# A two-layer encoder trunk on one core: x loaded first, modulation blocks pair by pair, norms summed on all partitions by TensorE, modulation sums held behind the norms

## The chip, the core and the metric

The kernel runs on one core of one Trainium2 chip. The metric is the device time of one execution in microseconds (us), from runs on the chip; smaller is better. The engines are named as the profile names them: PE is TensorE's matrix product and PEld its weight load, DVE is VectorE, ACT is ScalarE, POOL is GpSimd, SP is SyncE, which here only issues DMAs, in order.

## The reference

A sequence of 256 tokens of width 2048 (float32) goes through two layers, and then through a last norm with a gain. In each layer every sub-layer is modulated by six vectors that come from one conditioning vector `c`:

```python
cond = silu(c)
mod = cond @ w_ada[l] + b_ada[l]            # 2048 x 12288: six vectors of 2048
sh_a, sc_a, g_a, sh_m, sc_m, g_m = split(mod, 6)

h = rmsnorm(x) * (1 + sc_a) + sh_a
proj = h @ w_in[l]                          # queries, keys, values, latents
...                                         # 4 differential heads, 8 latent heads
x = x + g_a * (concat(out_a, out_b) @ w_o[l])

h = rmsnorm(x) * (1 + sc_m) + sh_m
x = x + g_m * (square(relu(h @ w_mlp_in[l])) @ w_mlp_out[l])     # 2048 -> 8192 -> 2048
```

`rmsnorm(x)` is `x * rsqrt(mean(x*x) + 1e-6)` over the 2048 features of a token. The two latent vectors of the attention (512 and 256 wide) have a norm with a gain as well.

## The kernel before

**Layout.** `x` stays in on-chip memory for the whole kernel as 16 tiles of 128 features by 256 tokens (features on partitions). Two neighbouring tiles make a *pair*; loops over features run over 8 pairs. A weight matrix comes in blocks of 128 partitions by 2048 columns (1 MiB), or in smaller ones.

**Precision by two parts.** A float32 number is written as hi + lo, both in a format that TensorE takes at its full rate. `weights` (L131) loads a raw block, ACT writes hi (L140), DVE writes lo = raw - hi (L141); the products are hi by hi, hi by lo and lo by hi (`mac`, L173). Raw blocks take turns in 5 buffers, hi and lo in 4 each. In layer 0's first product, six of the eight pairs (`WHOLE`) skip the split and use a float32 product (L233), of which the trace records two per tile; their weights load straight into hi and lo buffers (L222).

**The modulation.** `w_ada` is 192 blocks of 1 MiB. Each is multiplied by `cond` and summed along its columns by one DVE operation (L291), whose result is 128 entries of one of the six vectors; a small operation adds the bias (L305, L307). A block uses one of the 5 raw buffers. `ada` (L310) loads and sums at the place where it stands. Elsewhere a block is loaded now and then: each call of `weights` adds `rate` to a credit, loads a block for each whole credit, and queues the sums of the blocks loaded earlier behind its own last subtraction, by a dependency that only orders instructions (`after`, L294).

**The start.** `setup` (L323) loads `c` and small tables, issues four modulation blocks, `x` in four DMAs, sums up the squares of `x` (ACT squares, DVE adds them up, L470 and L471), and then issues ten more blocks (`LEAD`). The vectors sh_a and sc_a take 32 blocks, four for each pair. In `norm_then_by_k` (L528) the loop over the pairs asks for the blocks that its pair needs and that are not there yet (`ada_need`), modulates the pair, and multiplies it with its rows of `w_a` for all 12 column tiles, which accumulate in 6 PSUM banks. Between the pairs of layer 0 stand pieces of set-up work (`fills`: the relative bias and the rotary tables).

**The norm.** `rstd` (L474) turns sums of squares into 1/rms. The squares, tokens on columns, are the stationary operand and a single column of ones is multiplied with them (L482): the result has tokens on partitions, 128 x 1 for each half. ACT takes the root (L486), DVE the reciprocal of 2 columns (L487) and the product with the identity (L491), and TensorE multiplies this diagonal by ones (L492), which puts the 256 values on all partitions, in PSUM. The norms read it there, the first of the kernel reads a copy in on-chip memory (L534). It is called nine times: for four norms over `x` inside the layers, four latent norms and the last one.

**The modulated pair.** `modulated` (L495): DVE forms x times sc times 1/rms (L502), ACT adds sh and rounds to hi (L503), DVE adds sh and subtracts hi (L504). For a whole pair ACT writes the sum in float32 as well (L508).

**The order** of instructions on each engine is set when the program is built, by a planner that goes by the order of the program and its own estimate of when inputs and buffers are ready. Every engine then works through its own list in order.

Of the kernel before, what the change touches and what calls it, by code (L numbers as in the profile page):

```python
# [92 lines left out]
LEAD = 10  # L93
# [7 lines left out]
class Trunk:  # L101
    def __init__(self, ctx, tc, io):
        self.nc, self.tc, self.io = tc.nc, tc, io
        pool = lambda name, bufs, **k: ctx.enter_context(tc.tile_pool(name=name, bufs=bufs, **k))
        self.cp = pool("cp", 1)
        self.wp = pool("wp", 4)
        self.up = pool("up", 40)
        self.tp = pool("tp", 6)
        self.sp = pool("sp", 8)
        self.pp = pool("pp", 8, space=bass.MemoryType.PSUM)  # L110
        self.ada_todo, self.ada_here, self.rate, self.credit = [], [], 0.0, 0.0
        self.n = 0
# [18 lines left out]
    def weights(self, src, width=2048):  # L131
# [11 lines left out]
        self.ada_sums(ins)  # L143
# [179 lines left out]
    def setup(self):  # L323
# [132 lines left out]
    def sumsq(self, acc, val, alone=False):  # L456
# [8 lines left out]
        if acc is None:  # L465
            t = self.u("acc")
            nc.scalar.activation(t, val, AF.Square)
            return [t[:, 0], t[:, 1], t]
        t = self.t("sqx")
        nc.scalar.activation(t, val, AF.Square)  # L470
        nc.vector.tensor_tensor(acc[2], acc[2], t, ALU.add)  # L471
        return acc

    def rstd(self, acc, n):  # L474

        nc = self.nc
        ps = [self.bank("pn") for _ in range(2)]
        r = self.s("rms")
        acc = acc[:2] + acc[3:]
        for i, a in enumerate(acc):  # L480
            for t in range(2):
                nc.tensor.matmul(  # L482
                    ps[t][:, 0, :1], a[:, t * P : (t + 1) * P], self.ones[:, :1], start=i == 0, stop=i == len(acc) - 1
                )
        for t in range(2):
            nc.scalar.activation(r[:, t : t + 1], ps[t][:, 0, :1], AF.Sqrt, bias=self.eps, scale=1.0 / n)  # L486
        nc.vector.reciprocal(r, r)  # L487
        d = self.tp.tile([P, T], F32, tag="t", name=self.name("diag"))
        for t in range(2):
            c = slice(t * P, (t + 1) * P)  # L490
            nc.vector.tensor_scalar(d[:, c], self.ident, r[:, t : t + 1], None, ALU.mult)  # L491
        nc.tensor.matmul(ps[0][:, 1], self.ones, d, start=True, stop=True)  # L492
        return ps[0][:, 1]

    def modulated(self, r, k, sh, sc, whole):  # L495

        nc = self.nc
        t = self.t("ht")
        out = [self.parts("h") for _ in range(2)]
        for i, (hi, lo, _) in enumerate(out):  # L500
            c = slice(k + i, k + i + 1)
            nc.vector.scalar_tensor_tensor(t[:, i], self.x[:, k + i], sc[:, c], r, ALU.mult, ALU.mult)  # L502
            nc.scalar.activation(hi, t[:, i], AF.Identity, bias=sh[:, c])  # L503
            nc.vector.scalar_tensor_tensor(lo, t[:, i], sh[:, c], hi.bitcast(F32), ALU.add, ALU.subtract)  # L504
        if whole is not None:
            f = self.u("hf")
            for i in range(2):
                nc.scalar.activation(f[:, i], t[:, i], AF.Identity, bias=sh[:, k + i : k + i + 1])  # L508
                whole.append(f[:, i])
        return out  # L510
# [17 lines left out]
    def norm_then_by_k(self, l, acc, sh, sc, src, n, nwhole, fill=(), early=()):  # L528
# [445 lines left out]
```

## Time and profile before

| what | value |
|---|---|
| median of three runs | 2258.67 us (2252.15 to 2260.86) |
| the profiled execution | 2257.36 us |
| its span, first to last instruction | 2255.5 us |
| PE busy | 2191.2 us, 97% |
| DVE busy | 1668.4 us, 74% |
| ACT busy | 1124.8 us, 50% |
| moved by DMA | 585.57 MB, 260 GB/s on average |

The median is over unprofiled runs; the span and everything below it come from the one profiled execution. A busy time is a sum over the whole span, in which stages with different limits lie side by side. Rows of groups read: line, engine, operation, out<-in with the shapes, count | busy us, mean ns of one | idle time of the engine just before them, with what ended it. Rows of the timeline read: start, length, engine, line, operation, and in brackets the idle time before it and what ended it.

### The profile page before, as it was taken

To read this page: it belongs to the slowest core of one execution; us is meant where nothing else is said; L and a number is where in the kernel's file an instruction comes from. 1 tells how busy PE (TensorE), PEld (TensorE's weight loads), DVE (VectorE), ACT (ScalarE), POOL (GpSimd) and SP (SyncE) were. 2 spreads that over 40 slices of the span, in tenths; PEclk is the share of its full clock that TensorE was granted. 3 is DMA by queue.
4 is the path that set the end of the run, shared out by engine and by line. 5 is a ranking of instruction groups with operands and counts; after the bars stand their busy time and mean duration, and the time that the engine had idled before them with its cause. 6 is when DMAs were issued, how large, how long until landed. Compare 5 with 4: busy or idle time off the path is not lost.

```text
span 2255.5 us, 33717 instructions
## 1 busy us (share of the span) xinstructions
PE 2191.2 (97%) x13644; PEld 1967.6 (87%) x13644; DVE 1668.4 (74%) x2275; ACT 1124.8 (50%) x1660; POOL 1.9 (0%) x10
## 2 busy tenths in 40 slices
PE   3999999999999999999999999999999999999998
PEld 1899889998888888888889998999888888888887
DVE  7889878888888878878888786675655565565565
ACT  2655664455455355345445465544635534544553
POOL 0000000000000000000000000000000000000000
PEclk9999999999999999999999999999999999999999
DMA  9988678898888887888869766665555555555552
GB/s 365 357 314 319 257 278 313 309 340 326 300 317 311 302 316 288 332 315 315 301 249 345 265 231 225 237 227 183 203 186 186 177 201 187 187 187 187 187 187 75
DMA packets 85262, 585.57 MB, mean 260 GB/s; under 512 B 9457, under 2 KB 9841, under 8 KB 20593
## 3 DMA queue, kind: packets, MB, share of 16 engines
q1 hardware_dynamic: 85106, 583.42, 70.2%
q8 instruction: 107, 1.75, 0.3%
q14 instruction: 49, 0.40, 0.0%
HBM read 581.28 MB, written 2.10 MB: 259 GB/s over the span
## 4 chain that ended last, share of the span: by engine, by line
PE 94%; DVE 3%; DMA 1%; ACT 1%; issue 0%; SPq 0%; DVEq 0%; ACTq 0%
PE ps L196 38%; PE ps L197 20%; PE pk L176 5%; PE pk L177 5%; PE pk L178 5%; PE pk L233 3%; PE ps L177 3%; PE ps L176 3%; PE ps L178 3%; PE pv L249 1%; PE pv L247 1%; PE pv L248 1%; DVE ada L291 1%; PE po L828 1%; PE psm L863 1%; PE pom L880 1%
## 5 line engine op out<-in xcount | busy, mean ns | idle before, releaser
L141 DVE TENSOR_TENSOR lo<-raw,hi 128x1024 fp32r<-128x1024 f32 (+1 forms) x728 | 861.4, 1185 | 452.7 <-ACT hi L140 450.4
L140 ACT ACTIVATE hi<-raw 128x1024 fp32r<-128x1024 f32 (+1 forms) x728 | 746.9, 1028 | 855.8 <-PE ps L196 563.4
L196 PE MATMUL ps<-hid,hi 128*128 128x512 f32 x2048 | 721.2, 397 | 0.0
L196 PE MATMUL ps<-h,hi 128*128 128x512 f32 x1664 | 584.9, 396 | 0.0
L197 PE MATMUL ps<-hid,lo 128*128 128x256 f32 x2048 | 574.6, 281 | 0.0
L197 PE MATMUL ps<-h,lo 128*128 128x256 f32 x1664 | 466.9, 281 | 0.0
L196 PEld LDWEIGHTS ps<-hid,hi 128*128 128x128 f32 x2048 | 384.4, 188 | 93.7 <-DVE hid L170 0.5
L291 DVE SCALAR_TENSOR_TENSOR ada<-ada,cond 128x2048 f32<-128x2048 f32 x192 | 437.9, 2283 | 6.9 <-ACT cond L335 6.9
L197 PEld LDWEIGHTS ps<-hid,lo 128*128 128x128 f32 x2048 | 386.9, 189 | 0.0
L196 PEld LDWEIGHTS ps<-h,hi 128*128 128x128 f32 x1664 | 312.2, 188 | 74.9
L197 PEld LDWEIGHTS ps<-h,lo 128*128 128x128 f32 x1664 | 314.4, 189 | 0.0
L176 PE MATMUL pk<-h,hi 128*128 128x256 f32 x752 | 213.4, 288 | 3.5 <-ACT h L503 3.5
L177 PE MATMUL pk<-h,hi 128*128 128x256 f32 x752 | 214.3, 286 | 0.2 <-DVE h L504 0.2
L178 PE MATMUL pk<-h,lo 128*128 128x256 f32 x752 | 214.1, 285 | 0.0
L734 DVE SCALAR_TENSOR_TENSOR x<-ps,mod,x 128x256 f32<-128x256 f32 x224 | 108.2, 483 | 61.1 <-PE ps L197 56.9
L176 PEld LDWEIGHTS pk<-h,hi 128*128 128x128 f32 x752 | 146.0, 197 | 5.1 <-ACT h L503 5.1
L177 PEld LDWEIGHTS pk<-h,hi 128*128 128x128 f32 x752 | 146.5, 195 | 0.4 <-DVE h L504 0.4
L178 PEld LDWEIGHTS pk<-h,lo 128*128 128x128 f32 x752 | 146.4, 195 | 0.0
L233 PE MATMUL pk<-hf,w 128*128 128x256 f32 x288 | 65.9, 390 | 18.2 <-DMA w<-in_w_a 18.2
L233 PEld LDWEIGHTS pk<-hf,w 128*128 128x128 f32 x288 | 56.4, 197 | 27.1 <-ACT h L503 18.9
L746 ACT ACTIVATE relu<-sum 128x512 f32<-128x512 f32 x52 | 32.9, 632 | 69.9 <-DVE sum L741 69.9
L176 PE MATMUL ps<-h,hi 128*128 128x256 f32 x192 | 55.6, 289 | 0.0
(207 smaller groups left out, 2474.2 us busy)
## 6 DMA issues: line engine op xcount, KB each, us to landing
raw<-in_w_m SPq DMA_DIRECT2D x232, 1024.0 KB, 4.9
ada<-in_w_ada SPq DMA_DIRECT2D x192, 1024.0 KB, 5.0
raw<-in_w_ob SPq DMA_DIRECT2D x24, 1024.0 KB, 5.7
raw<-in_w_m SPq DMA_DIRECT2D x32, 768.0 KB, 4.6
raw<-in_w_dv SPq DMA_DIRECT2D x16, 1024.0 KB, 5.1
raw<-in_w_a SPq DMA_DIRECT2D x20, 768.0 KB, 6.3
raw<-in_w_t SPq DMA_DIRECT2D x12, 1024.0 KB, 5.1
w<-in_w_a SPq DMA_DIRECT2D x24, 384.0 KB, 5.8
```

Source lines behind the costliest of these rows:

```text
L140: nc.scalar.activation(hi, v, AF.Copy)
L141: ins = nc.vector.tensor_tensor(lo, v, hi.bitcast(F32), ALU.subtract)
L176: mm(ps, hi, x[0], start=first, stop=False, skip_group_check=shared)
L177: mm(ps, hi, x[1], start=False, stop=False, skip_group_check=shared)
L178: mm(ps, lo, x[0], start=False, stop=last, skip_group_check=shared)
L196: mm(ps.rearrange("p a b -> p (a b)"), hi, both, start=k == 0, stop=False)
L197: mm(ps[:, 0], lo, x, start=False, stop=k == nk - 1)
L233: self.nc.tensor.matmul(ps, w[i][:, j * P : j * P + P], whole[i], start=first, stop=last, skip_group_check=True)
L247: mm(ps, xh, hi, start=first and k == 0, stop=False)
L291: ins = nc.vector.scalar_tensor_tensor(w, w, 1.0, self.cond, ALU.mult, ALU.mult, accum_out=acc[:, i : i + 1])
L734: self.nc.vector.scalar_tensor_tensor(x, ps[i][:, j], g[:, m + i : m + i + 1], x, ALU.mult, ALU.add)
L746: self.nc.scalar.activation(r, ps, AF.Relu)
```

## The change

1. `setup` issues the four DMAs of `x` first and then four modulation blocks. The ten blocks of `LEAD` are not loaded there any more; each pair's blocks come when the loop over the pairs reaches it.
2. The squares of `x` in `setup` are kept as 16 tiles and not added up on DVE.
3. `rstd` makes all 128 columns of ones the stationary operand and multiplies the squares with it, 256 columns at a time: the sum lands on all partitions at once. The root and the reciprocal work on 128 x 256, and the result stays in on-chip memory, in one of the six buffers named "t". The diagonal and its product are gone, and so is the copy for the first norm.
4. `modulated`: DVE multiplies x by 1/rms only, ACT applies scale and shift together, once rounded to hi and once in float32 (for every pair now), and DVE subtracts the two.
5. In the first pair after a norm, the modulation sums that `weights` queues are ordered behind the last subtraction of that pair's modulation, and no longer behind the subtraction of the weights (`hold`).

```diff
-LEAD = 10
...
+        self.hold = None
...
-        self.ada_sums(ins)
+        self.ada_sums(self.hold or ins)
...
-        self.ada(4)
         for q in range(4):
             nc.sync.dma_start(self.x[:, 4 * q : 4 * q + 4], io["xT"][:, 4 * q : 4 * q + 4])
-        acc = None
+        self.ada(4)
+        acc = []
         for k in range(0, NK, 2):
-            acc = self.sumsq(acc, self.x[:, k : k + 2])
-        self.ada(LEAD)
+            t = self.u("sq")
+            nc.scalar.activation(t, self.x[:, k : k + 2], AF.Square)
+            acc += [t[:, 0], t[:, 1]]
         return acc
...
     def rstd(self, acc, n):
         nc = self.nc
-        ps = [self.bank("pn") for _ in range(2)]
-        r = self.s("rms")
-        acc = acc[:2] + acc[3:]
+        ps = self.bank("pn")[:, 0]
         for i, a in enumerate(acc):
-            for t in range(2):
-                nc.tensor.matmul(
-                    ps[t][:, 0, :1], a[:, t * P : (t + 1) * P], self.ones[:, :1], start=i == 0, stop=i == len(acc) - 1
-                )
-        for t in range(2):
-            nc.scalar.activation(r[:, t : t + 1], ps[t][:, 0, :1], AF.Sqrt, bias=self.eps, scale=1.0 / n)
+            nc.tensor.matmul(ps, self.ones, a, start=i == 0, stop=i == len(acc) - 1)
+        r = self.tp.tile([P, T], F32, tag="t", name=self.name("rstd"))
+        nc.scalar.activation(r, ps, AF.Sqrt, bias=self.eps, scale=1.0 / n)
         nc.vector.reciprocal(r, r)
-        d = self.tp.tile([P, T], F32, tag="t", name=self.name("diag"))
-        for t in range(2):
-            c = slice(t * P, (t + 1) * P)
-            nc.vector.tensor_scalar(d[:, c], self.ident, r[:, t : t + 1], None, ALU.mult)
-        nc.tensor.matmul(ps[0][:, 1], self.ones, d, start=True, stop=True)
-        return ps[0][:, 1]
+        return r

     def modulated(self, r, k, sh, sc, whole):
         nc = self.nc
         t = self.t("ht")
+        f = self.u("hf") if whole is not None else self.t("hf")
         out = [self.parts("h") for _ in range(2)]
         for i, (hi, lo, _) in enumerate(out):
             c = slice(k + i, k + i + 1)
-            nc.vector.scalar_tensor_tensor(t[:, i], self.x[:, k + i], sc[:, c], r, ALU.mult, ALU.mult)
-            nc.scalar.activation(hi, t[:, i], AF.Identity, bias=sh[:, c])
-            nc.vector.scalar_tensor_tensor(lo, t[:, i], sh[:, c], hi.bitcast(F32), ALU.add, ALU.subtract)
+            nc.vector.tensor_tensor(t[:, i], self.x[:, k + i], r, ALU.mult)
+            for z in (hi, f[:, i]) if whole is None else (f[:, i], hi):
+                nc.scalar.activation(z, t[:, i], AF.Identity, bias=sh[:, c], scale=sc[:, c])
+            ins = nc.vector.tensor_tensor(lo, f[:, i], hi.bitcast(F32), ALU.subtract)
...
-        return out
+        return out, ins
...
     def norm_then_by_k(self, l, acc, sh, sc, src, n, nwhole, fill=(), early=()):
         r = self.rstd(acc, D)
-        if early:
-            ps, r = r, self.tp.tile([P, T], F32, tag="t", name=self.name("rstd"))
-            self.nc.scalar.activation(r, ps, AF.Copy)
...
-            h += self.modulated(r, k, self.mod[l, sh], self.mod[l, sc], whole)
+            new, ins = self.modulated(r, k, self.mod[l, sh], self.mod[l, sc], whole)
+            h += new
+            self.hold = None if p else ins
             self.by_k(banks, [src[l, p, b] for b in range(2)], h, k, NK, 2 * n, whole)
+            self.hold = None
```

More of the change, by code (lines that the diff above doesn't have):

```diff
@@ L467, in sumsq @@
             nc.scalar.activation(t, val, AF.Square)
-            return [t[:, 0], t[:, 1], t]
+            self.acc2 = t
+            return [t[:, 0], t[:, 1]]
         t = self.t("sqx")
         nc.scalar.activation(t, val, AF.Square)
-        nc.vector.tensor_tensor(acc[2], acc[2], t, ALU.add)
+        nc.vector.tensor_tensor(self.acc2, self.acc2, t, ALU.add)
         return acc
@@ L501, in modulated @@
             c = slice(k + i, k + i + 1)
[L502 to L504 removed]
+            nc.vector.tensor_tensor(t[:, i], self.x[:, k + i], r, ALU.mult)
+            for z in (hi, f[:, i]) if whole is None else (f[:, i], hi):
+                nc.scalar.activation(z, t[:, i], AF.Identity, bias=sh[:, c], scale=sc[:, c])
+            ins = nc.vector.tensor_tensor(lo, f[:, i], hi.bitcast(F32), ALU.subtract)
         if whole is not None:
[L506 to L509, printed above, removed]
[L510 removed]
+            whole += [f[:, 0], f[:, 1]]
+        return out, ins
     def latent(self, vals, g):
```

## The prediction, made before the run

> **What bounds the kernel now.** I read the profile page first, then what TensorE waits for, then busy time by stretch, and last the timelines of the first 120 us and of the norms. The page: TensorE is busy for 2191.2 of 2255.5 us, so only 64 us of idle time can be won, beside the time it runs at a lower clock.
>
> ```profile
> span 2255.5 us, 33717 instructions
> PE 2191.2 (97%) x13644; PEld 1967.6 (87%) x13644; DVE 1668.4 (74%) x2275; ACT 1124.8 (50%) x1660; POOL 1.9 (0%) x10
> ```
>
> The list of TensorE's waits names the places (total us, times, longest):
>
> ```profile
> PE pk L233 <- DMA w<-in_w_a: 18.2, 1, 18.2
> PE pn L482 <- DVE acc L471: 15.3, 1, 15.3
> PE pn L492 <- DVE diag L491: 7.3, 4, 2.7
> ```
>
> The first two lie in the first 49 us; the third is the chain of the four big norms. By stretch (length, then busy us of PE, PEld, DVE, ACT, POOL, then granted clock, DMA share, GB/s):
>
> ```profile
> 10.50:28.00 17.50, 1.87 (x8) 1.78 (x8) 16.13 (x19) 5.89 (x10) 0.00 (x0) 1.00 1.01 423
> 28.00:48.00 20.00, 1.19 (x2) 0.50 (x2) 19.46 (x32) 3.90 (x10) 0.00 (x0) 1.00 0.98 394
> 28.00:62.00 34.00, 14.48 (x53) 11.82 (x53) 32.07 (x54) 9.94 (x21) 0.00 (x0) 1.00 0.90 350
> 62.00:118.00 56.00, 56.00 (x257) 48.49 (x257) 50.20 (x96) 33.32 (x58) 0.53 (x1) 1.00 0.94 361
> 118.00:168.00 50.00, 49.84 (x376) 48.36 (x376) 42.74 (x52) 25.46 (x35) 0.00 (x0) 1.00 0.83 317
> 168.00:250.00 82.00, 78.26 (x582) 73.88 (x582) 76.54 (x143) 45.48 (x83) 0.00 (x0) 1.00 0.78 295
> 428.00:441.00 13.00, 9.02 (x51) 8.25 (x50) 11.03 (x20) 5.31 (x11) 0.00 (x0) 0.74 0.86 302
> ```
>
> Until 48 us TensorE has nothing to do; from 62 us it is full. But VectorE is 90% busy from 28 to 62 us and 93% from 168 to 250 us, and DMA tops out near 423 GB/s. The start can be shortened only as far as these two allow. The last row is a norm: TensorE idle for 4 of 13 us, at a mean clock of 0.74.
>
> **The start, step by step.** These rows of the timeline (start, length) set it:
>
> ```profile
> 9.90 31.64 SPq L283 DMA_DIRECT2D ada<-in_w_ada  x10
> 41.59 15.53 SPq L222 DMA_DIRECT2D w<-in_w_a  x10
> ...
> 16.73 0.63 ACT L467 ACTIVATE acc<-x 128x512 f32<-128x512 f32 x1 [6.23 <-DMA x<-in_xT]
> ...
> 48.72 13.23 PE L233 MATMUL pk<-hf,w 128*128 128x256 f32 x48 [18.19 <-DMA w<-in_w_a]
> ...
> 61.92 10.61 PE L233 MATMUL pk<-hf,w 128*128 128x256 f32 x48
> ...
> 118.05 10.52 PE L233 MATMUL pk<-hf,w 128*128 128x256 f32 x48
> ```
>
> Before, the ten LEAD blocks sit in SP's in-order queue ahead of the first weights of w_a, which are issued at 41.59. Removing LEAD lets SP issue x (4 DMAs), 4 blocks, 4 weight tiles, then each pair's 4 blocks and 4 tiles. Nothing on POOL's queue moves. x used to land behind four 1 MiB blocks, with its first quarter used at 16.73; without that 4.2 MB at 423 GB/s (9.9 us) it is there at about 7. The four blocks land when the old x did: 16.7 us plus the other three quarters, 1.6 MB at 423 GB/s, 20.4 us. The last of them needs one sum (2.28 us), a small add and ACT's pass (0.50): the first product can start at about 25, say 26 to be safe with the norm's own steps between the sums. Its four weight tiles (1.6 MB, 3.7 us) start to land just behind the blocks. So TensorE could start 48.7 - 26 = 22.7 us earlier.
>
> How much is kept? From 61.92 to 118.05 TensorE needs 14.0 us per pair, bias work included. Per pair, DMA must now bring four blocks and 1.57 MB, 5.77 MB, 13.6 us at 423 GB/s: just enough. VectorE is tighter. It worked 16.13 + 32.07 + 50.20 + 42.74 + 76.54 = 217.7 us from 10.5 to 250. The durations for what changes (busy, mean ns):
>
> ```profile
> L291 DVE SCALAR_TENSOR_TENSOR ada<-ada,cond 128x2048 f32<-128x2048 f32 x192 | 437.9, 2283 | 6.9 <-ACT cond L335 6.9
> ...
> L471 DVE TENSOR_TENSOR acc<-acc,sqx 128x512 f32<-128x512 f32 x7 | 4.8, 691 | 0.6
> ...
> L502 DVE SCALAR_TENSOR_TENSOR ht<-x,mod,pn 128x256 f32<-128x256 f32 x48 | 21.1, 475 | 2.4 <-PE pn L492 2.2
> ...
> L449 DVE TENSOR_TENSOR cc<-cc,rr 128x256 f32<-128x256 f32 x1 | 0.4, 426 | 0.0
> L448 DVE TENSOR_SCALAR cc<-rr 128x256 f32<-128x256 f32 x1 | 0.3, 293 | 0.0
> ...
> L307 DVE TENSOR_TENSOR mod<-macc,vec 128x2 f32<-128x2 f32 x64 | 9.8, 154 | 0.2
> ...
> L740 ACT ACTIVATE sum<-ps 128x256 f32<-128x256 f32 x104 | 38.1, 367 | 0.0
> L503 ACT ACTIVATE h<-ht,mod 128x256 fp32r<-128x256 f32 x64 | 29.4, 500 | 37.7 <-DVE ht L502 37.5
> ```
>
> The seven adds of squares go (-4.8; TensorE does them in 16 products of two records each, 2 x 10.52 / 48 = 0.44 us, while it has nothing else). Each of the 16 modulated tiles of this stage trades two operations of 0.48 for two of 0.43 (-1.7). In three norms (the first and two latents) the 2-column reciprocal and the diagonal (0.16 + 0.48) give way to one reciprocal of 128x256.
>
> **The reciprocal** of 256 columns is in no row; the nine of 2 columns are (least, median, largest ns):
>
> ```profile
> L487 DVE RECIPROCAL rms<-rms x9: 158/159/167, 28.4 to 2244.8; 128x2 f32<-128x2 f32 x9
> ```
>
> From below it costs what the cheapest 256-column operation does, 0.29 us. From above: the slowest one against the 154 ns of a 2-column add is 6.5 ns for a column, 256 x 6.5 + 160 = 1.8 us. By the median it is 2.5 ns a column, 0.8 us. The rows are coarse (5 ns decide), so I take the middle of the last two, 1.3, and keep 0.29 and 1.8.
>
> So VectorE's work until 250 us becomes 217.7 - 4.8 - 1.7 - 1.9 + 3.9 = 213.2 us, and it can begin only when the first block lands, at 12.9 (20.4 less three blocks of 2.5). If it keeps the density of 168 to 250, 76.54/82 = 0.933, it needs 228.5 us and ends at 241.4: the stage gains 8.6 us. With the density of 28 to 48 (0.973) the gain is 18; with the mean of 28 to 250 (201.6/222 = 0.908) it is 2.3. I take 8.6, because the long dense stretch is the nearest thing to what comes.
>
> **The norms.** One of them, last square to first product:
>
> ```profile
> 1159.96 0.42 ACT L462 ACTIVATE sqa<-x 128x256 f32<-128x256 f32 x1 [0.26 <-DVE x L734]
> ...
> 1160.71 2.28 DVE L291 SCALAR_TENSOR_TENSOR ada<-ada,cond 128x2048 f32<-128x2048 f32 x1
> ...
> 1162.92 0.16 DVE L487 RECIPROCAL rms<-rms 128x2 f32<-128x2 f32 x1
> ...
> 1163.74 1.19 PE L492 MATMUL pn<-diag,ones 128*128 128x256 f32 x2 [2.71 <-DVE diag L491]
> ...
> 1166.05 1.65 PE L176 MATMUL pk<-h,hi 128*128 128x256 f32 x6 [1.11 <-ACT h L503]
> ```
>
> A modulation sum runs on VectorE just when the reciprocal is due; the hold puts it behind the first pair's last subtraction. The new chain from the end of the last square: product with ones 0.71 (the fastest of the old broadcast products, 0.67, below), root 0.37, reciprocal 1.3, multiply 0.43, ACT 0.50, with some 0.05 between each: 3.6 us. Here it was 1166.05 - 1160.38 = 5.7, a gain of 2.1. The other three:
>
> ```profile
> 429.19 0.81 ACT L462 ACTIVATE sqa<-x 128x256 f32<-128x256 f32 x2 [5.15 <-DVE x L728]
> 434.44 1.65 PE L176 MATMUL pk<-h,hi 128*128 128x256 f32 x6 [1.17 <-ACT h L503]
> ...
> 1514.38 0.70 ACT L462 ACTIVATE sqa<-x 128x256 f32<-128x256 f32 x2
> 1517.05 0.67 PE L492 MATMUL pn<-diag,ones 128*128 128x256 f32 x2 [1.16 <-DVE diag L491]
> 1518.89 1.65 PE L176 MATMUL pk<-h,hi 128*128 128x256 f32 x6 [1.18 <-ACT h L503]
> ...
> 2243.44 0.42 ACT L462 ACTIVATE sqa<-x 128x256 f32<-128x256 f32 x1 [4.69 <-DVE x L734]
> 2246.91 4.61 DVE L896 TENSOR_TENSOR x<-x,pn 128x1024 f32<-128x1024 f32 x4 [1.37 <-PE pn L492]
> ```
>
> They took 4.4, 3.8 and (to the final multiply) 3.05 us; the new ones take 3.6, 3.6 and 2.55: gains of 0.8, 0.2 and 0.5. Together 3.6 us; with the reciprocal at 0.29 it is 7.6, at 1.8 it is 1.6.
>
> **What I cost at nothing.** The second ACT pass (64 tiles less the 12 of the whole pairs that had one, 52 x 0.50 = 26 us) hides in ACT's idle time, 7.7 of 13 us in the norm's stretch. On the path it only delays the first remainder by 0.5 us, and the six leading hi-hi products (1.65) cover that; without this cover each norm pays 0.5. The held sums delay the weight subtractions queued behind them on VectorE and the release of their raw buffers, for which SP waits; one pair's converted weights lie ahead, 72 products of 49.84 / 376 = 0.13 us, so nothing waits for 9.5 us. The four latent norms change off TensorE's path, behind other columns' products; without that cover each pays a long reciprocal, 1.3. The root now stays in one of six "t" buffers for the whole stage and a pair takes two instead of one; that leaves two pairs ahead, 19 us of products.
>
> **The sum.** 8.6 + 3.6 = 12.2 us less. The profiled execution took 2257.36 us around its span of 2255.5, 1.3 under the median of 2258.67; 2257.36 - 12.2 = 2245.2, and against the median 2246.5. I say 2246. Its own range, from the ends: 18 + 7.6 gives 2233, 2.3 + 1.6 gives 2255.
>
> **The rivals.** *The reciprocal is slow* (2250, no change that can be told). At 1.8 us it takes 2 us from the norms, and 1.5 us more work in three norms, at 0.933, 1.6 from the start: 8.6 us less than now. For it: even the fastest of the nine takes longer than the mean add. Against: the median speaks for half of it. The Trainium skill, page "VectorE: DVE Perf Modes", section "First, the fixed hardware budget", says that a reciprocal is an iterative divide with a repeat count of 8. If that means eight cycles per column at that page's 0.96 GHz, my estimate from it is 256 x 8 / 0.96 = 2.1 us plus start-up, and the time would be about 2253. No row here shows a reciprocal long enough to decide.
>
> *VectorE takes it all* (2256). Blocks now arrive just in time, and VectorE's order is fixed: a sum placed ahead of bias work waits for its block and holds the bias up. The sums of 62 to 118 us:
>
> ```profile
> L291 DVE SCALAR_TENSOR_TENSOR ada<-ada,cond 128x2048 f32<-128x2048 f32 x10 | 22.7, 2284 | 0.0
> ```
>
> The other work of that stretch is (50.20 - 22.7) / 4 = 6.9 us a pair; with four sums, 9.1, a pair would want 16.0 us of VectorE beside 14.0 of TensorE. For it: no slack while the bias is built. Against: five raw buffers, so sums may lag by a block or two, and at 16.0 us a pair the sixth still starts at 26 + 13 + 4 x 16 = 103. If it happens the start gains nothing and the norms 3 us.
>
> *Pair by pair becomes one after the other* (slower). If each pair's loads, sums, modulation and products fail to overlap, a pair takes four blocks 9.9 + sum 2.28 + modulation 1.4 + products 10.5 = 24.1 us; the sixth pair starts at 26 + 5 x 24.1 = 146.5 instead of 118.05, a loss of 28.5, less 3.6 from the norms, and 2283 in the end. It decides from 19.1 us per pair on ((118.05 + 3.6 - 26) / 5). For it: LEAD's blocks were the cushion. Against: weights for two pairs and five raw buffers may run ahead, and both queues were kept full before.
>
> *The clock stays up* (2238). TensorE ran the first products after the norm slowly (granted clock 0.74 in that stretch). At half speed for half of 13 us it loses about 3.4 us, and three such norms some 8. A new chain of 3.6 us with wide products at its head instead of 1-column ones might avoid the drop. The Trainium skill's page "TensorE: Matmul & The Clock Gate", section "What's actually happening", has the clock halved after an idle window of about 3.4 us; by that rule a gap this long is a coin toss; with all three drops gone the time would be the same 2238.
>
> **How the numbers follow.** Half a per cent, 11.3 us, is about what a measurement of this kernel can tell from no change. My forecast 0.44 (0.33 of it beyond 0.5%, the rest within), the slow reciprocal 0.14 and VectorE takes it all 0.10 (both within), one after the other 0.20 (slower, with any overlap between 19.1 and 24.1 us a pair), the clock stays up 0.12 (faster). So faster 0.45, same 0.35, slower 0.20. The range 2233 to 2264 takes in all but most of the slow case.
>
> **What would show it.** Right: the first L233-like product near 26 us, pairs every 14 to 16 us, the sixth starting near 105, no sum between the last square and the reciprocal of a norm, 3.6 us from square to product. Wrong: TensorE waiting in every pair on weights or modulated tiles, VectorE idle behind late blocks, a reciprocal of 2 us or more, new waits after 120 us where VectorE was already full.

## The result, and the profile after

The change makes the kernel a little slower: 2261.78 us in the median of 19 runs (2255.22 to 2268.70), against 2255.19 us for the kernel before in 19 runs beside them (2249.05 to 2263.20). The ratio is 1.0025, with a 95% interval of 1.0014 to 1.0037. The forecast was 2246. The difference of 6.6 us is below half a per cent, but it has the other sign. The profiled execution took 2262.86 us, its span is 2261.0.

The page of the kernel after, and the head of what TensorE waits for in it (total us, times, longest):

```profile
span 2261.0 us, 33630 instructions
PE 2201.8 (97%) x13602; PEld 1975.1 (87%) x13602; DVE 1665.8 (74%) x2250; ACT 1152.9 (51%) x1702; POOL 1.9 (0%) x10
```

```profile
PE pk L233 <- ACT hf L497: 24.5, 6, 9.5
PE pk L176 <- ACT h L497: 12.7, 4, 4.2
PE psc L788 <- DVE mx L789: 2.9, 3, 1.5
```

The wait of 18.2 us for the first weights and the one of 15.3 us for the sum of squares are gone. In their place TensorE waits six times for ACT's float32 tiles, once per whole pair: 9.5 us ahead of the first and 15.0 us ahead of the other five. It is also busy for 10.6 us longer than before (2201.8 against 2191.2) with 42 instructions fewer, and its mean granted clock is 0.986 instead of 0.994. Busy time by stretch, with the columns as in the prediction, shows where:

```profile
10.50:28.00 17.50, 8.19 (x32) 6.59 (x30) 12.02 (x15) 5.27 (x9) 0.00 (x0) 0.87 1.02 424
28.00:62.00 34.00, 29.30 (x114) 24.52 (x114) 29.63 (x52) 13.32 (x24) 0.00 (x0) 0.86 0.99 400
62.00:118.00 56.00, 48.59 (x184) 40.08 (x185) 44.47 (x77) 26.73 (x46) 0.53 (x1) 0.85 0.77 294
118.00:168.00 50.00, 44.80 (x308) 41.66 (x307) 42.70 (x63) 23.48 (x35) 0.00 (x0) 0.97 0.79 292
```

The third row tells most. From 62 to 118 us TensorE got through 257 recorded products before and 184 now, at a granted clock of 0.85 where it was 1.00. Yet VectorE is busy for only 44.5 of these 56 us (50.2 before) and DMA moves 294 GB/s (361 before): no engine is full, so the work waits for itself in a circle. The starts of the whole pairs in the timeline of TensorE:

```profile
28.19 13.40 PE L233 MATMUL pk<-hf,w 128*128 128x256 f32 x48 [9.50 <-ACT hf L497]
44.46 12.11 PE L233 MATMUL pk<-hf,w 128*128 128x256 f32 x48 [2.75 <-ACT hf L497]
...
82.30 13.65 PE L233 MATMUL pk<-hf,w 128*128 128x256 f32 x48 [3.10 <-ACT hf L497]
102.72 13.68 PE L233 MATMUL pk<-hf,w 128*128 128x256 f32 x48 [3.10 <-ACT hf L497]
123.17 7.04 PE L233 MATMUL pk<-hf,w 128*128 128x256 f32 x25 [3.10 <-ACT hf L497]
```

The first pair starts 20.5 us earlier than before (28.19 for 48.72). After that a pair comes every (123.17 - 28.19) / 5 = 19.0 us instead of every 14 us (before: 48.72, then 61.92 to 118.05), and the sixth starts 5.1 us later than before. The 48 products that the trace records for a pair (two for each float32 product) take 12.0 to 13.7 us instead of 10.5; only the first pair was as slow before (13.23). The last row above is cut off by its window: the whole pair takes 12.01 us.

One turn of the circle, in order of time, for the pair that starts at 102.72 (its first column counts us from the start of the span):

```profile
95.61 0.75 DVE L495 TENSOR_TENSOR ht<-x,rstd 128x256 f32<-128x256 f32 x2
96.02 0.39 PE L427 MATMUL pb<-oh,lscl 128*128 128x512 f32 x1
98.75 0.15 DVE L305 SCALAR_TENSOR_TENSOR mod<-macc,vec 128x2 f32<-128x2 f32 x1
99.23 0.39 PE L427 MATMUL pb<-oh,lscl 128*128 128x512 f32 x1
99.66 2.38 ACT L429 ACTIVATE bias<-pb 32x512 f32<-32x512 f32 x4 [9.69 <-PE pb L427]
102.06 0.60 ACT L497 ACTIVATE hf<-ht,mod,mod 128x256 f32<-128x256 f32 x1
```

VectorE has x times 1/rms ready at 96.4 and the last modulation vector at 98.9. But in ACT's list the four copies of the relative bias (L429) stand ahead of the pair's modulation (L497). These copies wait for the bias products (L426, L427), and these stand in TensorE's list behind the products of the pair before. So ACT stands still for 9.69 us, then copies for 2.38 us, then makes the tile, and TensorE, which has done its last bias product at 99.62, waits 3.10 us. In the kernel before, ACT's list had it the other way round: the float32 tiles of the pair at 90.05 are written before the bias copies that lie under the pair at 76.05. ACT's timeline of before:

```profile
77.38 0.89 ACT L508 ACTIVATE hf<-ht,mod 128x256 f32<-128x256 f32 x2
...
81.58 2.38 ACT L428 ACTIVATE bias<-pb 32x512 f32<-32x512 f32 x4
```

Up to the last product of this stage (it starts at 178.3 after, at 169.0 before) the account is: the first pair 20.5 earlier; TensorE's five waits between pairs 15.0; the five later pairs at a lower clock 11 (12.11 + 12.31 + 13.65 + 13.68 + 12.01, less five times 10.55); two waits of 1.6 and 0.5 for the last two pairs. That makes 7.6 of the 9.3 us that the stage ends later; the other 1.7 are not accounted for. The two profiled spans differ by less, 5.5 us: the attention takes 0.2 us longer, and 4.0 us come back behind it.

The norm whose rows stand in the prediction for before, now:

```profile
1167.81 0.42 ACT L463 ACTIVATE sqa<-x 128x256 f32<-128x256 f32 x1 [0.26 <-DVE x L725]
1168.28 0.70 PE L481 MATMUL pn<-sqa,ones 128*128 128x256 f32 x2 [0.25 <-ACT sqa L463]
1169.02 0.47 ACT L483 ACTIVATE rstd<-pn,eps 128x256 f32<-128x256 f32 x1 [0.79 <-PE pn L481]
1169.53 1.75 DVE L484 RECIPROCAL rstd<-rstd 128x256 f32<-128x256 f32 x1 [0.88 <-ACT rstd L483]
1171.31 1.43 DVE L495 TENSOR_TENSOR ht<-x,rstd 128x256 f32<-128x256 f32 x4
1171.77 0.60 ACT L497 ACTIVATE h<-ht,mod,mod 128x256 fp32r<-128x256 f32 x1 [2.28 <-DVE ht L495]
1172.42 1.65 PE L176 MATMUL pk<-h,hi 128*128 128x256 f32 x6 [3.44 <-ACT h L497]
1174.22 2.28 DVE L291 SCALAR_TENSOR_TENSOR ada<-ada,cond 128x2048 f32<-128x2048 f32 x1
```

The hold does what it says: no sum lies between the last square and the reciprocal, and the next one comes at 1174.22, behind the pair's modulation. But the chain from the end of the last square (1168.23) to the first product takes 4.2 us, not 3.6, and the reciprocal is the largest piece of it. In the norm at 439 the chain is longer still, since VectorE subtracts weights (L141, 0.89 us) between the reciprocal and the multiplication; the hold does not order these. The four chains (the last one to the final multiply) took 4.44, 5.67, 3.81 and 3.05 us before and take 4.98, 4.19, 4.38 and 3.08 now: together 0.3 us less.

### The profile page after: what moved, and what is told of

Read it like the earlier page. It is cut to its first block, busy times and chain, and to the rows that moved or that the text cites. A ratio compares the mean times of both kernels' runs of the same rounds, so it can differ in the third digit from the quotient of the medians.

```text
span 2261.0 us, 33630 instructions
## 1 busy us (share of the span) xinstructions
PE 2201.8 (97%) x13602; PEld 1975.1 (87%) x13602; DVE 1665.8 (74%) x2250; ACT 1152.9 (51%) x1702; POOL 1.9 (0%) x10
## 4 chain that ended last, share of the span: by engine, by line
PE 91%; DVE 5%; ACT 2%; issue 1%; DMA 1%; DVEq 0%; ACTq 0%
PE ps L196 37%; PE ps L197 19%; PE pk L176 4%; PE pk L177 4%; PE pk L178 4%; PE pk L233 3%; PE ps L178 3%; PE ps L176 3%; PE ps L177 3%; DVE ada L291 2%; PE pv L249 1%; PE pv L247 1%; PE pv L248 1%; DVE lo L141 1%; DMA raw<-in_w_m 1%
## 5 line engine op out<-in xcount | busy, mean ns | idle before, releaser
L141 DVE TENSOR_TENSOR lo<-raw,hi 128x1024 fp32r<-128x1024 f32 (+1 forms) x728 | 860.5, 1185 | 448.2 <-ACT hi L140 446.3
L197 PE MATMUL ps<-h,lo 128*128 128x256 f32 x1664 | 466.7, 280 | 0.0
L291 DVE SCALAR_TENSOR_TENSOR ada<-ada,cond 128x2048 f32<-128x2048 f32 x192 | 437.6, 2283 | 10.8 <-DMA ada<-in_w_ada 10.7
L176 PEld LDWEIGHTS pk<-h,hi 128*128 128x128 f32 x752 | 146.2, 197 | 14.1 <-ACT h L497 14.1
L233 PE MATMUL pk<-hf,w 128*128 128x256 f32 x288 | 77.2, 436 | 24.5 <-ACT hf L497 24.5
L233 PEld LDWEIGHTS pk<-hf,w 128*128 128x128 f32 x288 | 63.6, 223 | 37.9 <-ACT hf L497 26.7
L178 PE MATMUL ps<-h,lo 128*128 128x256 f32 x192 | 55.6, 290 | 1.0 <-DVE lo L141 1.0
```

The lines of the kernel that those rows point to most:

```text
L141: ins = nc.vector.tensor_tensor(lo, v, hi.bitcast(F32), ALU.subtract)
L176: mm(ps, hi, x[0], start=first, stop=False, skip_group_check=shared)
L178: mm(ps, lo, x[0], start=False, stop=last, skip_group_check=shared)
L197: mm(ps[:, 0], lo, x, start=False, stop=k == nk - 1)
L233: self.nc.tensor.matmul(ps, w[i][:, j * P : j * P + P], whole[i], start=first, stop=last, skip_group_check=True)
L291: ins = nc.vector.scalar_tensor_tensor(w, w, 1.0, self.cond, ALU.mult, ALU.mult, accum_out=acc[:, i : i + 1])
```

## The experiments

Four readings stood against each other, all of them about the loop over the first six pairs: that the order of ACT's list makes it a chain; that supply does (blocks from memory, and their sums on VectorE); that the other half of the change does, the new norms and ACT's second pass; and that the clock is a cost by itself. Three marks of a run are better than its total: the start of the sixth pair, the start of the stage's last product, and the end of the last square ahead of the layer's second norm, since a later stretch, in which the edits change no more than one norm (from that square to the last one of layer 0), took 723.7 to 734.9 us in the fourteen profiled executions. Each mark comes from one profiled execution. All times of other kernels are medians, with the ratio to runs of the kernel before on the same chip and its 95% interval.

| kernel | first pair | sixth pair | last product of the stage | time, ratio to before |
|---|---|---|---|---|
| before | 48.72 | 118.05 | 169.0 | 2255.19 |
| after | 28.19 | 123.17 | 178.3 | 2261.78, 1.0025 (1.0014 to 1.0037) |
| order of the start alone | 28.58 | 124.17 | 177.9 | 2266.23, 1.0048 (1.0029 to 1.0067) |
| norms alone | 45.97 | 114.70 | 167.6 | 2259.50, 1.0011 (0.9994 to 1.0028) |
| next pair's modulation first | 27.80 | 112.4 | 182.3 | 2272.23, 1.0078 (1.0057 to 1.0100) |
| the same for the first six only | 27.70 | 112.3 | 176.8 | 2268.90, 1.0062 (1.0044 to 1.0080) |
| TensorE kept busy | 27.89 | 115.06 | 171.3 | 2255.26, 1.0008 (0.9993 to 1.0022) |
| short sums | 25.25 | 120.69 | 174.2 | 2262.93, 1.0026 (1.0013 to 1.0039) |
| first six ahead and short sums | 25.37 | about 95 | 149.2 | 2238.03, 0.9922 (0.9901 to 0.9942) |
| two bias pieces in the head | 47.79 | 112.09 | 164.2 | 2247.07, 0.9963 (0.9949 to 0.9978) |

### Which half of the change

The first kernel is the one before with only the order of the start changed:

```diff
-        self.ada(4)
         for q in range(4):
             nc.sync.dma_start(self.x[:, 4 * q : 4 * q + 4], io["xT"][:, 4 * q : 4 * q + 4])
+        self.ada(4)
...
-        self.ada(LEAD)
```

> The kernel before with only the order of the start changed: x first, no ten blocks ahead. Old norms, old modulation, no hold. Theories A and B both expect the pair loop to run at 18 to 21 us per pair as in the changed kernel, and 2259 to 2267 us. Theory C (the rewritten norm and modulation, with a second ScalarE pass and a 1.75 us reciprocal, are what costs): the start's gain shows unspoilt here, 2235 to 2248 us.

The second is the one after, with the old order and the ten blocks put back:

```diff
+        self.ada(4)
         for q in range(4):
             nc.sync.dma_start(self.x[:, 4 * q : 4 * q + 4], io["xT"][:, 4 * q : 4 * q + 4])
-        self.ada(4)
...
+        self.ada(10)
         return acc
```

> The changed kernel with the old order of the start put back: four blocks, then x, then ten blocks ahead. So only norms, modulation and hold are new. Theories A and B: the pairs run at 14 us again from about 48 us on, the four big norms cancel to within 2 us, 2251 to 2259 us. Theory C: slower than before by 6 us or more, 2261 to 2268 us.

What TensorE waits for with the order alone:

```profile
PE pk L233 <- ACT hf L507: 26.3, 6, 7.7
```

The stretch from 62 to 118 us with the norms alone:

```profile
62.00:118.00 56.00, 56.00 (x258) 48.52 (x257) 47.79 (x96) 34.06 (x58) 0.53 (x1) 1.00 0.89 342
```

The order alone has the waits, the 19.1 us per pair ((124.17 - 28.58) / 5) and the late end of the stage (177.9). With the new norms, the second ACT pass and the old order, TensorE is full at full clock, with 258 products where before has 257, and the stage ends 1.4 us earlier than before (167.6). So the loss in the loop belongs to the order of the start, and the norms cost it 1.3 us at most (the first pair starts 2.75 us earlier than before). That the norms alone still come out no faster has another place: from the stage's last product to the square ahead of the second norm it takes 265.5 us, against 261.0 before. There TensorE waits for ACT's copies of the keys (5.8 us in three waits, 3.1 before) and of the queries (2.3), in an order of the attention's work that the planner chose differently; four of the fourteen programs show this (264.6 to 266.9 us: the norms alone, and the three below that put the modulation ahead with full sums); the others lie between 259.8 and 261.9. Why the planner goes over was not found out.

### What makes the pairs a chain

Here the next pair's modulation is put ahead of the bias work, in the order of the program:

```diff
-        for p in range(8):
+        def mod(p):
...
+        ahead = mod(0)
+        for p in range(8):
+            new, ins, whole = ahead
...
             self.hold = None
+            if p < 7:
+                ahead = mod(p + 1)
             if fill:
                 fill.pop(0)()
```

> The changed kernel with one difference: the next pair is asked for and modulated ahead of this pair's piece of set-up work (bias), in the order of the program. Amount of work, blocks and bytes are the same. Theory A (ScalarE's order: the four bias copies, which wait for TensorE's bias products, stand in ScalarE's list ahead of the next pair's modulation, so each pair pays about 3.1 us of waiting and a half-rate start): the waits of 3.1 us for hf go, the sixth pair starts near 103 us instead of 123.2, the clock from 62 to 118 us is 0.97 or more instead of 0.85, and the time is 2236 to 2248 us. Theory B (supply: VectorE's sums and the landing of the blocks set the 19 us per pair): the order on ScalarE changes nothing, the sixth pair still starts near 123, 2258 to 2266 us.

The expected gain did not come; the kernel is slower than after. ACT's waits between 28 and 128 us show the order working and what takes its place. After:

```profile
ACT bias L429 <- PE pb L427: 36.4, 4, 9.9
```

With the next pair first:

```profile
ACT hf L497 <- DVE mod L305: 19.2, 5, 9.2
ACT bias L429 <- PE pb L427: 14.9, 4, 5.0
```

The wait behind the bias copies falls from 36.4 to 14.9 us, but the modulation now waits 19.2 us for its vectors from VectorE. A pair takes (112.4 - 27.8) / 5 = 16.9 us instead of 19.0, with the bias products now inside the pairs, and 70 us instead of 55 pass from the sixth pair to the end of the stage. There TensorE waits for something else:

```profile
PE pk L176 <- ACT hi L140: 10.4, 2, 5.3
```

ACT's high parts of the next weights come late. Its list shows why, at the first of the two waits:

```profile
129.12 0.60 ACT L497 ACTIVATE h<-ht,mod,mod 128x256 fp32r<-128x256 f32 x1 [4.10 <-DVE mod L305]
...
131.10 3.45 ACT L140 ACTIVATE hi<-raw 128x1024 fp32r<-128x1024 f32 x4
```

The first of these high parts belong to `w_d`, whose raw block was issued at 111.40 and landed after 4.7 us. But in ACT's list they stand behind the seventh pair's tiles, which now come first and wait for their vectors (4.10 us here, 4.48 at the second wait). In the kernel after they are made at 129.13, ahead of these tiles. So it is the same fault with the parts exchanged. The next kernel does the same only for the pairs without a split (`if p + 1 < nwhole`).

> As the run with the next pair modulated first, but only among the six float32 pairs; the seventh and eighth pair keep the changed kernel's order, so that their blocks don't take the raw buffers of the w_d weights. Theory A (ScalarE's order costs the loop 2 us a pair, and the rest of the earlier run's loss came from the last two pairs): the sixth pair starts near 112 us again, and the stretch from there to the last product of the stage takes some 55 us as in the changed kernel instead of 70; 2247 to 2255 us. If the early modulation itself costs what was lost: 2265 us or more.

That wait is gone and the stage ends at 176.8, 1.5 us before that of after. This is still far from the expectation: the sixth pair starts 11 us earlier, and most of it is lost again behind it, where one wait of 6.6 us for ACT's next tile stands. The stretch from 28 to 62 us shows what the early pairs run into:

```profile
28.00:62.00 34.00, 27.62 (x106) 22.62 (x105) 26.11 (x43) 8.77 (x17) 0.00 (x0) 0.85 1.01 416
```

DMA is full at 416 GB/s, and the sums of the blocks, each of which has to land first, come just before the modulation: supply, by the blocks or by their sums. The total is worse than that of after (1.0062 for 1.0025) although the stage ends earlier; the slower attention order (266.9 us for 261.2) accounts for 5.7 us, and the rest of some 4 us is open.

Supply by itself is tested with sums that read 64 of the 2048 columns, for all 32 blocks of the two vectors of the loop. This leaves out most of these sums; the blocks are loaded in full.

```diff
+            some = (l, g) in ((0, 0), (0, 1))
+            v = w[:, :64] if some else w
...
-                w, w, 1.0, self.cond, ALU.mult, ALU.mult, accum_out=acc[:, i : i + 1]
+                v, v, 1.0, self.cond[:, :64] if some else self.cond, ALU.mult, ALU.mult, accum_out=acc[:, i : i + 1]
```

> The changed kernel, but the 32 blocks of the first shift and scale are summed over 64 of their 2048 columns (part of the modulation is left out, so the output is not the reference's). All loads, all waits on them and the order on ScalarE stay; VectorE has 2.1 us less work per block, 8.5 us per pair. Theory A (ScalarE's list: the bias copies stand ahead of the next pair's modulation): the wait of 3.1 us per pair and the half-rate products stay, pairs of 18 to 20.4 us, sixth pair at 117 to 123 us. Theory B (VectorE's sums pace the loop): pairs fall to 14 to 16 us, sixth pair at 100 to 108 us.

```profile
62.00:118.00 56.00, 48.94 (x192) 40.49 (x192) 28.90 (x97) 27.82 (x48) 0.53 (x1) 0.88 0.80 305
...
100.06 13.58 PE L233 MATMUL pk<-hf,w 128*128 128x256 f32 x48 [3.10 <-ACT hf L499]
```

VectorE has 15.6 us less to do in this stretch (28.90 for 44.47 us) and the loop stays as it was, only 1 to 3 us earlier, as the first sums are short too: the same wait of 3.10 us, the same slow 13.58 us of products, 19.1 us per pair, 2262.93 us in all. VectorE's load is not what holds the kernel after. With the short sums and the first six pairs ahead, both together:

> The same short sums (part of the modulation left out) in the kernel that modulates the next of the six pairs ahead of the bias piece. If the next limit behind ScalarE's order was the sums: the waits of that kernel for the modulation (20.3 us in all, 9.5 of them at the start) fall to the first one, the six pairs run at 14 us and the stage's last product ends near 160 us instead of 176.8. If it was the blocks' landing: no more than 3 us are won, 173 us or later.

```profile
62.00:118.00 56.00, 56.00 (x292) 49.56 (x291) 36.05 (x108) 38.49 (x62) 0.70 (x1) 1.00 1.00 410
```

TensorE is full at full clock with 292 products, a pair takes (95 - 25.37) / 5 = 13.9 us, the stage ends at 149.2 and the kernel takes 2238.03 us. Each of the two edits alone gained nothing; together they gain 1% over after, some 23 us (0.9922 for 1.0025). So two limits lie one behind the other: ACT's order first, and as soon as it is gone, the sums that the modulation waits for. It was the sums and not yet the blocks' landing: from 28 to 62 us DMA is as full with the short sums (422 GB/s) as without them (416), and TensorE gets 135 products through instead of 106. DMA would be the third limit.

### What the clock costs

Three products of 128x512 into a bank that nothing reads follow the bias work of each of the first five pairs, so that TensorE does not idle there:

```diff
+            if nwhole and p < 5:
+                ps = self.bank("warm").rearrange("p a b -> p (a b)")
+                for _ in range(3):
+                    self.nc.tensor.matmul(ps, self.ones, self.cond[:, :512], start=True, stop=True)
```

A first version of it has one more difference: it also leaves out three of the seven parts in which 2 pi is subtracted from the rotary angles.

> The changed kernel with three float32 products of ones by cond (512 columns, into a bank nobody reads, some 2.6 us at the full clock) behind the bias products of each of the first five pairs, where TensorE sits idle for 3.1 us. The wait itself stays. Theory A with the clock as its second half (a pair's 48 products take 12.3 to 13.7 us instead of 10.5 because they start at half rate): the products go back to some 10.6 us, the clock in 62 to 118 us to 0.97 or more, pairs to 17 us, and the time falls by 8 to 14 us to about 2250. If the long products come from weights that land late, the dummies change nothing, or cost up to 2.6 us per pair: 2261 to 2274 us.

> The changed kernel with the three dummy products behind each of the first five pairs and nothing else different (the earlier run also left out three of the seven steps that reduce the rotary angles, 1.3 us of VectorE's work, in the tables' set-up). Theory A with the clock as its second half: as before, 48 products in 10.6 us and pairs of 17.7 us, 2252 to 2258 us. If the missing steps made the difference: 2258 to 2263 us.

From the version without that difference:

```profile
62.00:118.00 56.00, 53.35 (x224) 41.94 (x224) 49.94 (x91) 30.82 (x52) 0.53 (x1) 1.00 0.86 330
...
97.35 10.63 PE L233 MATMUL pk<-hf,w 128*128 128x256 f32 x48 [0.90 <-ACT hf L497]
```

The clock is 1.00, the products of a pair take 10.63 us again and a pair 17.4 us ((115.06 - 27.89) / 5). The stage ends 7.0 us sooner than in after, at 171.3; the first version has 170.1. In the profiles, then, keeping TensorE busy is worth 7.0 of the 9.3 us that the stage ends later. The totals, 2255.26 us (1.0008) and 2254.69 (0.9997), say the same less sharply: against the 1.0025 of after they are some 4 and 6 us lower, and the interval of the clean version just overlaps that of after. The chain itself stays (a wait of 0.90 us is left behind the dummies, and a pair still takes 3 us more than before).

How long a wait is does not by itself decide whether the next products are slow. In the kernel with the order of the start alone:

```profile
65.69 10.63 PE L233 MATMUL pk<-hf,w 128*128 128x256 f32 x48 [3.28 <-ACT hf L507]
...
103.58 13.11 PE L233 MATMUL pk<-hf,w 128*128 128x256 f32 x48 [3.80 <-ACT hf L507]
124.17 10.63 PE L233 MATMUL pk<-hf,w 128*128 128x256 f32 x48 [3.80 <-ACT hf L507]
```

Two of its five waits left the clock at 1.00, and so did one of 3.01 us with the first six ahead and short sums. What else decides was not found out. On top of the first six pairs ahead the same products give nothing:

> Both: the six float32 pairs modulated ahead, and the three dummy products. If the two halves are separate, TensorE's order of waiting first and the clock second, the pairs run at 15 to 16 us and the sixth starts near 105 us: 2240 to 2248 us. If supply (VectorE's sums behind landing blocks) is the next limit, the dummies find no idle time to fill and delay the products: pairs of 17 us or more, 2250 to 2258 us.

The stage ends at 176.9 (176.8 without them) and the time is 2268.52 us, above both expectations: the dummies fill the idle time, but it is the modulation's vectors that are late there.

### Taking work out of the loop instead

In the last 17.5 us before the first product of after (10.5 to 28), TensorE is busy for 8.2, ACT for 5.3 and VectorE for 12.0 us. Here the setup of the relative bias and its first two pieces are done in `setup`, and not between the pairs:

```diff
-FILL = "lb|0|1|2|3|r"
+FILL = "l|2|3|r"
...
+        self.bias_setup()
+        self.bias_part(0)
+        self.bias_part(1)
         self.ada(4)
```

> The changed kernel with the bias set-up and two of the four bias pieces ahead of the first sums in the order of the program, where VectorE waits from 3.4 to 14.3 us for the first block. Two pairs of the loop then have no bias work. Theory A: a pair without a bias eviction between it and the next has neither the wait nor the half-rate start, 14 us or less instead of 19 to 20; the first pair starts at up to 6 us later, as the pieces overrun the idle stretch. Net 4 to 8 us faster than the changed kernel, 2253 to 2258 us. Theory B: pairs without bias work still take 17 us or more.

```profile
47.79 13.15 PE L233 MATMUL pk<-hf,w 128*128 128x256 f32 x48 [6.80 <-ACT hf L500]
...
100.28 10.63 PE L233 MATMUL pk<-hf,w 128*128 128x256 f32 x48 [0.71 <-ACT hf L500]
112.09 10.63 PE L233 MATMUL pk<-hf,w 128*128 128x256 f32 x48 [1.18 <-ACT hf L500]
```

```profile
62.00:118.00 56.00, 54.11 (x248) 46.55 (x247) 50.38 (x87) 22.92 (x39) 0.53 (x1) 1.00 1.01 410
```

The first pair starts as late as in the kernel before (19.6 us later than after, where up to 6 were expected), but the later ones follow every 12.9 us ((112.09 - 47.79) / 5; the last two are 11.8 apart), DMA is full at 410 GB/s, and the stage ends at 164.2: 14.1 us sooner than after and 4.8 sooner than before. At 2247.07 us it beats both (0.9963, 0.9949 to 0.9978). Less work in the loop is not all of it: the two pieces of bias work that are left lie between pairs 14.1 and 14.0 us apart, without a wait. ACT's list has the tiles of the pair at 89.05 from 81.80 on, ahead of the bias copies at 89.25, as in the kernel before. With the later start the vectors are there in time for that order, as I read it; this was not tested by itself. Three pieces in the head, and all four:

> As the run with two bias pieces in the head, with three. If pieces in the head cost less than in the loop (there they cost the 3.5 us of products, 3.1 of waiting and some 3 us at half rate): another 2 to 5 us less, 2243 to 2246 us. If the head is already full, the first pair starts 5.6 us later for each piece and the loop, now paced by DMA, wins nothing: 2247 to 2251 us.

> All four bias pieces in the head: no bias work in the loop at all. Theory A: no wait on the modulation beyond 1.2 us per pair anywhere in the loop, pairs at 10.6 to 14 us. The first pair starts near 58 us. If head and loop trade evenly the time is that of the run with two pieces, 2245 to 2250 us; if the sums queued behind the pieces delay the blocks' buffers, DMA stands idle in the head and it is 2252 us or more.

They start the first pair at 58.59 and 68.23 and end the stage at 168.3 and 173.8; the times are 2254.47 us (0.9995, 0.9982 to 1.0009), slower than either expectation, and 2261.46 us (1.0026, 1.0010 to 1.0041). Each further piece delays the first pair by about 10 us, where 5.6 were expected, and makes the loop faster by less. Two is the best of the numbers tried.

## Why the prediction was wrong

**What bounds the kernel.** Right about where the time lay: both early waits went. (VectorE was 94% busy from 28 to 62 us before, 32.07 of 34, and not 90%; nothing hangs on it.) Wrong in the conclusion that the start "can be shortened only as far as" VectorE and DMA allow. From 62 to 118 us neither is full; the bound was the order of ACT's list, an engine that the prediction counted as idle and did not follow instruction by instruction.

**The first product.** Forecast at 26, measured at 28.19. The third sum stands in VectorE's list behind the reciprocal; that waits for the root, the root for a table load of 1.28 us on ACT, and the load for TensorE's sum of squares, which ends at 18.69: its 16 products take 8.95 us, where the 0.44 us for each make 7.0. So the last of the four sums starts at 24.80 and not at about 20. That is a miss of 2 us, and not the one that matters.

**How much is kept? This is the step that failed.** It took the whole stage as one pile of VectorE work at a density of 0.933, and a pair as 14 to 16 us. VectorE's density came out at 0.87 from 28 to 62 us and at 0.79 from 62 to 118, and cutting its work by 15.6 us left the total where it was. The forecast gain of 8.6 us in the stage became a loss of 9.3. What the sum left out: with LEAD's blocks loaded, the next pair's modulation stood ahead of the bias copies in ACT's list (that the planner put it there because its vectors were due earlier is inferred; the run with two bias pieces in the head agrees, where a later start brought this order back). Without them the bias copies stand first in that list, and products, bias products, copies and modulation run one after the other.

**VectorE takes it all** (2256). Its time is nearer than the forecast's, but its mechanism is not what happened: no sum held the bias work up, the bias work held the modulation up. It does show one layer down, once ACT's order is mended.

**Pair by pair becomes one after the other** (2283). This rival names what happened, with "LEAD's blocks were the cushion" and with the right point of decision: it put the break-even at 19.1 us per pair, and at a measured 19.0 the kernel is just slower. Its links were others, and fewer: loads and sums do run ahead, while the bias copies, which it did not have, close the chain. The argument against it, that weights and raw buffers may run ahead, was true and beside the point, since the tile that was late was neither.

**The clock stays up** (2238). It went the other way. Behind the three later norms inside the layers the clock fell as before: granted 0.50 to 0.53 in the first 3.2 to 3.6 us of products, before and after. The prediction looked for the clock only there and did not price it for gaps in the loop. The five waits of about 3 us cost 11 us of slow products beside their own 15.0.

**The norms.** Forecast 3.6 us, measured 0.3. The mechanism was right, with the hold and without the diagonal; four sizes were off. The reciprocal takes 1.75 us, near the far end of the range and not in its middle (1.3); root 0.47 for 0.37; ACT's pass 0.60 for 0.50; and the root starts 0.74 after the product, for 0.71. In each chain these three make 0.45 + 0.10 + 0.10 = 0.65 us more than the sum had. Only the norm at 1168, whose sum the hold moves out of the way, gained clearly, 1.5 us (5.67 to 4.19); two others lost half a microsecond each. So *The reciprocal is slow* was right on the size: with 1.8 us it left 1.6 us of gain in the norms, and it would have been the better value to take. The row that gives it was in the prediction, the 167 ns of the slowest 2-column reciprocal, but so were the median (159) and the fastest (158), which give half of it or less; these rows were too coarse to choose by. The Trainium skill's page "VectorE: DVE Perf Modes", section "First, the fixed hardware budget", has a repeat count of 8 for a reciprocal; the estimate from it, 2.1 us and more, is too long by a fifth against the measured 1.75, yet nearer than 1.3.

**What was costed at nothing.** The second ACT pass, the held sums, the buffers "t" and the latent norms: the run with the norms alone bears this out for the loop (full TensorE, stage 1.4 us earlier). What it did not allow for is that the planner answers to new durations in places far off: 4.5 us in the attention of that run, from an order that no edit touched.

## What to carry to other kernels

Before blocks are taken out of a head start, read the in-order list of every engine between two steps of the loop, the mostly idle ones too: an eviction that waits for the end of this step and stands ahead of the next step's operand turns the loop into a chain, whatever the engines' loads. When a forecast rests on the load of one engine, work out as well the longest path through one turn of the loop, with gaps priced at their own length and at the slower products behind them. Work that sits between the steps can often be moved into the idle head; here two pieces of four were the right amount, and an early first product by itself was worth nothing.

## What the runs showed of the hardware

- A reciprocal of 128x256 in float32 took 1.75 us on VectorE in all nine norms, and one of 128x2 took 0.16: some 6.3 ns for each further column, where the multiplication of the same shape takes 0.42 us.
- ACT's pass with a shift per partition took 0.50 us for 128x256, and with scale and shift per partition 0.59. The Trainium skill, page "ScalarE: Activation LUTs", section "What ACT_TABLE_LOAD costs", has some 93 ns more for each such operand; these rows agree, and the prediction could have had the number from there.
- In the kernel after, waits of 2.75 to 3.10 us after bursts of 14 to 17 us were enough to slow the next products: 48 of them took 12.0 to 13.7 us for 10.5. With waits of 0.9 us (three dummy products in the gap) they took 10.63. The Trainium skill, page "TensorE: Matmul & The Clock Gate", section "What's actually happening", has the clock halved after an idle window of about 3.4 us; in the kernel after a shorter wait was enough in five pairs out of five, and in the kernel with the order alone waits of 3.28 and 3.80 us were not (10.63).
- DMA ran at 400 to 424 GB/s through whole stretches of 17 to 56 us, where blocks and weights were asked for early enough.
